# A planner's buffer choice by last reader, copies of x spread over eight blocks, and the next head's loads moved to mid-head, in a one-core hybrid layer

## The chip, the cores and the metric

One program runs on one core of a Trainium2 chip. The metric is the device time of one execution in microseconds (us), lower is better. The engines of the core work side by side: TensorE (PE, with its weight loads PEld), VectorE (DVE), ScalarE (ACT), GpSimd (POOL) and SyncE (SP), which here issues nearly all transfers. Each engine and each queue runs its own instructions strictly in their written order and waits on semaphores where data or a buffer is not ready.

## The reference, cut to what matters

One layer of a decoder over 512 prompt tokens and 64 sample tokens (T = 576 columns), model width 2048, all float32:

```python
proj = x @ w_in + b_in                      # 2048 -> 14352
(s5_u, s5_z, q, k, v, a_low, gla_z, ca, cb, cz, gates) = split(proj)
y_s5  = gelu(s5_mixer(s5_u, ...));  y_s5 = y_s5 * sigmoid(y_s5 @ w_glu + b_glu)
br_s5 = (y_s5 * silu(s5_z)) @ p_s5
o     = gla_mixer(q, k, v, a_low, ...)      # 4 heads, chunked linear attention with decay
br_gla  = (o * silu(gla_z)) @ p_gla
br_conv = (conv_mixer(ca, cb, ...) * silu(cz)) @ p_conv
out = (g_s5 * br_s5 + g_gla * br_gla + g_conv * br_conv) @ w_o     # g = sigmoid(gates)
h = alpha * x + out;  h = h + sigmoid(h @ w_pg) * (p @ w_pe)
return layer_norm(h), the mixers' new states
```

## The kernel before

Activations stand transposed, 128 channels by 576 tokens to a tile. Each large product is made of three products of parts: every operand is split into `hi` (a copy rounded to fp32r, by ACT on line 75) and `lo` (the rest, a subtraction by DVE on line 82), and hi*hi, hi*lo and lo*hi are summed in PSUM, in matmuls of 288 columns (line 435 for plain jobs, 464 for pairs of output blocks that use a seven-product scheme, 547 for the small `w_pe`).

`run_jobs` writes out the work unit by unit; a job is one block of 128 output channels. The order is: eight `s5_u` blocks, the `a` block, ten gate blocks (`NFILL`), 47 pairs for the rest of `w_in`, two quads of `w_pe`, eight `w_glu` blocks, 16 blocks each of `p_s5`, `p_conv` and `p_gla`, eight pairs of `w_o` and 16 blocks of `w_pg`. Weights arrive in four `raw` buffers (lines 352, 375) and, for a part of the pairs, in slots (line 359). Background work is written as Python generators that `pump` advances after each piece of matmuls: the S5 mixer (eight blocks, each `s5_block`, `s5_scan`, `s5_out`), the convolution tiles, the four GLA heads (`gla_head`), and the products y*z (`y_make`). A scheduler then orders each engine's instructions within dependences, so a transfer may be issued well before the place where it is written.

The S5 block b needs a turn through DRAM: line 951 stores a table of kernels to `kd` from a slot that line 970 frees at once, and the sixteen loads of line 967 read it back in a shifted layout for the matmuls of line 1044. Lines 985 and 1040 are the S5 state matmuls before and beside them. `s5_store_u` (line 842 on) empties the PSUM of an `s5_u` block into a slot by ACT and stores it to `ud`.

SBUF is managed as 71 slots of 128x576 (`NSLOT`), named `sl` in the profile. `alloc` takes the slot that stands first in a queue, and `free` puts a slot at its end; `free` is called as soon as the last reader has been written out, which may be a store (to `ud`, `kd`, `gd` for gates, `zd`, `gx` for the convolution's input, `qd` for q, k and v, `cd`, `yd`, `xd` and others). The slot's next writer then waits until that store has landed.

`x_out(k)` copies the k-th transposed block of x to DRAM (`xd`) for its use at the end of the layer: a store of its `hi` part by SP (line 1689), then an adding store of its `lo` part by POOL (line 1690). Eight are written out before the `a` job and eight before the last of the ten gate jobs.

`gla_head(h)` begins with `gla_load` (four transfers from `qd`, line 1238, and two steps of waiting) if its tiles have not been asked for; at the end of head h, line 1397, the tiles of head h + 1 are asked for where more than ten slots are free.

Of the kernel before, what the change touches and what calls it, by code (L numbers as in the profile page):

```python
# [25 lines left out]
NSLOT = 71  # L26
# [19 lines left out]
class K:  # L46
# [10 lines left out]
    def alloc(self, dt=F32):  # L57
        n = 0
        while not self.inbg and (not self.free_slots or n < 300 and self.bg and len(self.free_slots) <= self.reserve):
            self.force()  # L60
            n += 1
            assert n < 5000, ([e[1] for e in self.bg], [e[0].gi_frame.f_lineno for e in self.bg])
        i = self.free_slots.popleft()
        self.cnt += 1
        t = self.slots.tile([128, T], dt, name=f"sl{self.cnt}", tag=f"s{i}")
        self.owner[id(t)] = (i, t)
        return t

    def free(self, *ts):
        for t in ts:  # L70
            i, _ = self.owner.pop(id(t))
            self.free_slots.append(i)

    def act(self, out, in_, func=AF.Copy, **kw):
# [118 lines left out]
    def setup(self):  # L193
        nc, tc, ctx = self.nc, self.tc, self.ctx
        self.const = ctx.enter_context(tc.tile_pool(name="const", bufs=1))
        self.rawp = ctx.enter_context(tc.tile_pool(name="raw", bufs=4))
        self.hip = ctx.enter_context(tc.tile_pool(name="hi", bufs=6))
        self.lop = ctx.enter_context(tc.tile_pool(name="lo", bufs=6))
        self.dram = ctx.enter_context(tc.tile_pool(name="dram", bufs=1, space=DRAM))
        self.ps_mm = ctx.enter_context(tc.tile_pool(name="psmm", bufs=2, space=PSUM))  # L200
        self.ps_two = ctx.enter_context(tc.tile_pool(name="pstwo", bufs=1, space=PSUM))
        self.ps_aux = ctx.enter_context(tc.tile_pool(name="psaux", bufs=2, space=PSUM))
        self.slots = ctx.enter_context(tc.tile_pool(name="slots", bufs=1))
        self.free_slots = deque(range(NSLOT))
# [12 lines left out]
        nc.vector.memset(self.one1, 1.0)  # L217
        self.act(self.one1, self.one1)
# [102 lines left out]
    def run_jobs(self):  # L321
# [126 lines left out]
        def run_pair(u):  # L448
# [38 lines left out]
            if hooks is not None:  # L487
                hooks(p)
            self.pump(BG_PAIR * 3.2)

# [11 lines left out]
        for b, (k0, n) in enumerate(xblocks):  # L502
            g = k0 // HK
            for j in range(2):
                if k0 % HK == 0:
                    prep(2 * g + j)
                if k0 == 0:
                    pss[j] = self.ps_mm.tile([128, 1024], F32, name="mm")
                if j == 1 and b < 4:
                    self.turn_x(*xblocks[b + 1])  # L510
                ka, m, hi, lo = halves[2 * g + j][0]
                mms(pss[j], (k0, n, hi[:, k0 - ka:], lo[:, k0 - ka:]), X, KT, FULL)
                if b > 1:
# [11 lines left out]
        for u in range(first, nu):  # L525
# [11 lines left out]
            if kind == "quad":  # L537
                if before is not None:
                    before()
                xh, xl = xs()  # L540
                hv = halves.pop(u)
                for j in range(4):
                    ps = self.ps_mm.tile([128, 1024], F32, name="mm")
                    for k, (_, _, hi, lo) in enumerate(hv):
                        for lh, rh, a, b in ((hi, xh, k == 0, False), (hi, xl, False, False), (lo, xh, False, k == 1)):
                            for o, c, m in FULL:
                                nc.tensor.matmul(ps[:, o:o + m], lh[:, j], rh[k][:, c:c + m], start=a, stop=b)  # L547
                    evac(j, ps)
                    self.pump(BG_SHORT * 1.6)
                continue  # L550
# [8 lines left out]
            for z, (ka, m, hi, lo) in enumerate(hv):  # L559
                for c in range(0, m, 2):  # L560
                    mms(pss[ji], (ka + c, 2, hi[:, c:], lo if lo is None else lo[:, c:]), xs, nk,
                        PARTS[:1] if dual in (1, 2) else FULL)
                    if z < len(hv) - 1 or c < m - 2:
                        self.pump(rate * 1.6)
            if dual in (1, 2):
                kept.append((ji, xs, hv))
            if k0 + n == nk:
                if dual in (1, 2):
                    evac(pss[ji], 0)
                else:  # L570
                    evac(pss.pop(ji))
                if after is not None:
                    after()
            self.pump(rate * 1.6)
        nm = 0
# [265 lines left out]
    def s5_store_u(self, b, ps):  # L841
# [6 lines left out]
        self.nc.sync.dma_start(self.ud[b], t)  # L848
        self.free(t)
        self.u[b] = True  # L850
# [16 lines left out]
    def s5_block(self, b, st):  # L867
# [83 lines left out]
        nc.sync.dma_start(self.kd[b, :, 128:], kt[:, 128:256])  # L951
        self.free(t)
        if b < 7 and self.u[b + 1] is not None:
# [75 lines left out]
    def s5_out(self, b, st):  # L1029
# [27 lines left out]
        for s in range(8):  # L1057
            nc.sync.dma_start(dst[s], u[16 * s:16 * s + 16].rearrange("c (g n) -> c g n", g=8))
        self.free(t, u)
        yield 2.0  # L1060
# [180 lines left out]
    def gla_head(self, h):  # L1241
# [134 lines left out]
        for a in range(2):  # L1376
# [11 lines left out]
            for z in (2 * a + 1, 2 * a):  # L1388
                nc.gpsimd.dma_start(self.o[8][0, 2 * z:2 * z + 2, h].rearrange("s d v -> d s v"),
                                    s0[z][:, :512].rearrange("p (s v) -> p s v", s=2))  # L1390
                self.free(s0[z])
# [17 lines left out]
        for s in range(2):  # L1409
# [8 lines left out]
            nc.sync.dma_start(self.yd[1, 2 * h + s], y)  # L1418
            self.free(y)
            yield 0.1  # L1420
# [15 lines left out]
    def conv_g(self, n, ca, sig):  # L1436
# [16 lines left out]
        nc.sync.dma_start(self.gx[n, :, 576:880], g2[:, :304])  # L1453
        self.free(g, g2)

# [5 lines left out]
    def conv_tile(self, n):  # L1461
# [19 lines left out]
        nc.gpsimd.dma_start(self.o[9][0, :, 22:30, cs], tmp[:64, 256:384])  # L1481
        self.free(tmp)
        y = self.alloc()
# [20 lines left out]
        nc.sync.dma_start(self.cd[0, n], y)  # L1504
        self.free(y)
        yield 0.7
# [7 lines left out]
    def conv_norm(self):  # L1514
# [17 lines left out]
        for n in range(8):  # L1532
# [9 lines left out]
            nc.sync.dma_start(self.cd[1, n], y)  # L1542
            self.free(y)
            yield 1.4
# [10 lines left out]
        for n in range(8):  # L1555
# [7 lines left out]
            nc.sync.dma_start(self.yd[2, n], y)  # L1563
            self.free(y)
            yield 2.1
# [12 lines left out]
    def br_job(self, name, br, n, y, key, mode, extra=None, order=range(16)):  # L1578
# [20 lines left out]
        def evac(ps):  # L1599
# [6 lines left out]
            else:  # L1606
                self.add(self.A[n], self.A[n], g)
            self.free(g)
        self.job(w, n * 128, lambda: ([a for a, _ in y], [b for _, b in y]), evac, before)
        self.rates[id(self.jobs[-1])] = RATES[name]  # L1610

    def build(self):
# [22 lines left out]
        def evac_a(ps):  # L1635
# [3 lines left out]
            nc.sync.dma_start(self.ad, t)  # L1639
            self.free(t)  # L1640
            self.spawn(self.make_forms(), "forms")
        gates = deque([(1, n) for n in range(16)] + [(0, n) for n in range(16)] + [(2, n) for n in range(16)])

        def gate_one(br, n):
            def evac(ps):
# [3 lines left out]
                nc.sync.dma_start(self.gd[br, n], t)  # L1649
                self.free(t)  # L1650
            self.job(w_in, OFF["gates"] + br * D + n * 128, X, evac)
# [5 lines left out]
        def gate_pair(br, n):  # L1657
            col = OFF["gates"] + br * D + n * 128

            def evac(t0, X0, t1):  # L1660
# [4 lines left out]
                for z, t in enumerate((t0, t1)):  # L1665
                    nc.sync.dma_start(self.gd[br, n + z], t)
                self.free(t0, t1)
            return col, evac

        def z_pair(br, name, n):  # L1670
# [3 lines left out]
            def evac(t0, X0, t1):  # L1674
# [8 lines left out]
                for z, t in enumerate((t0, t1)):  # L1683
                    nc.sync.dma_start(self.zd[br, n + z], t)
                self.free(t0, t1, s0, s1)
            return col, evac
# [93 lines left out]
        def kqv_pair(n, col):  # L1780
            def evac(t0, X0, t1):
# [4 lines left out]
                for z, t in enumerate((t0, t1)):  # L1786
                    nc.sync.dma_start(self.qd[n + z], t)
                self.free(t0, t1)
            return col, evac
# [51 lines left out]
        def pe_quad(m):  # L1841
            def evac(j, ps):
                t = self.alloc()
                self.act(self.s2(t), self.v2(ps))
                nc.sync.dma_start(self.pd[4 * m + j], t)
                self.free(t)
            self.quad_job(self.i["w_pe"][0], 512 * m, parts(P), evac, lambda: self.need("p"))
# [102 lines left out]
        for n in range(0, 16, 2):  # L1950
            def evac(t0, X0, t1, n=n):
# [5 lines left out]
                for k, t in ((n, t0), (n + 1, t1)):  # L1957
                    if n < 12:
                        nc.sync.dma_start(self.hd[k], t)
                        self.free(t)  # L1960
                    else:
                        HL[k] = t
# [330 lines left out]
```

## Time and profile before

| what | value |
|---|---|
| median of three runs | 2302.80 us (2291.73, 2302.80, 2303.48) |
| the profiled execution's own time | 2296.74 us |
| its span, first to last instruction | 2294.8 us |
| PE busy | 2240.8 us, 16892 matmuls |
| DVE / ACT busy | 1797.1 / 1042.0 us |
| SP's queue | 329.16 MB in 422336 packets |
| mean granted clock of PE | 0.990 |

All stages are tables of matmuls with the rest beside them; PE is busy nearly throughout, so what matters is where it stands still and where its clock is halved behind such a halt. Stages by time from the span's start: loading and turning x to about 50 us; plain jobs with the S5 mixer to about 302 us; pairs of `w_in` with the convolution to about 1395 us; `w_glu`, `p_s5`, `p_conv` with the GLA heads to about 1700 us; `p_gla` and `w_o` to about 2045 us; `w_pg` and the layer norm to the end.

### The profile page before, as it was taken

How to read it: one execution, taken by the hardware profiler on the slowest of the kernel's cores; microseconds unless marked ns; L12 is line 12 of the kernel's file. 1: busy time of each engine (PE TensorE's matmuls, PEld its weight loads, DVE VectorE, ACT ScalarE, POOL GpSimd, SP SyncE). 2: the span in 40 equal slices, each digit the busy share in tenths (PEclk: the TensorE clock that was granted, in tenths of full speed). 3: DMA queues.
4: the chain of work that ended last, by engine and by line, in shares of the span. 5: the costliest groups of instructions: out<-in, count | busy, mean ns of one | idle time of the engine just before them, and what ended most of it. 6: DMA issues, size and time to landing. Idle time of an engine off the chain costs nothing.

```text
span 2294.8 us, 44332 instructions
## 1 busy us (share of the span) xinstructions
PE 2240.8 (98%) x16892; PEld 2195.0 (96%) x16892; DVE 1797.1 (78%) x3417; ACT 1042.0 (45%) x2058; POOL 69.7 (3%) x121
## 2 busy tenths in 40 slices
PE   8989999999999999999999999999999999999998
PEld 7979999999999999999999999998989999999996
DVE  6967877989898989999989779865653777774556
ACT  4444444454545455544545556563422334453221
POOL 0010010000000000000000000000110000000000
PEclk9999999999999999999999999999999999999998
DMA  7565574434444443444444467856878444464322
GB/s 214 148 150 133 137 183 140 119 111 137 125 130 120 126 137 119 140 124 131 119 137 123 135 193 261 263 180 191 261 224 219 124 130 141 153 209 130 95 84 83
DMA packets 430005, 348.86 MB, mean 152 GB/s; under 512 B 51198, under 2 KB 368314, under 8 KB 429776
## 3 DMA queue, kind: packets, MB, share of 16 engines
q1 hardware_dynamic: 422336, 329.16, 48.3%
q0 software_dynamic: 7456, 16.88, 3.4%
q8 instruction: 132, 2.16, 0.4%
q14 instruction: 81, 0.66, 0.1%
HBM read 263.74 MB, written 82.89 MB: 151 GB/s over the span
## 4 chain that ended last, share of the span: by engine, by line
PE 83%; issue 6%; DMA 5%; DVE 3%; ACT 2%; SPq 1%; POOL 0%; DVEq 0%; POOLq 0%; ACTq 0%
PE mm L464 30%; PE mm L435 27%; PE aux L464 22%; DVE sl L82 2%; PE mm L547 1%; DMA sl<-in_w_in 1%; PE aux L104 1%; ACT sl L75 1%; DMA kd<-sl 1%; DMA sl<-zd 1%; DVE lo L82 1%; PE two L104 1%; DMA sl<-in_x_prompt 1%; PE two L1040 0%; DVE sl L100 0%
## 5 line engine op out<-in xcount | busy, mean ns | idle before, releaser
L75 ACT ACTIVATE hi<-raw 128x512 fp32r<-128x512 f32 x800 | 501.7, 630 | 669.6 <-PE mm L435 249.1
L435 PE MATMUL mm<-sl,hi 128*128 128x288 f32 (+2 forms) x4000 | 723.1, 300 | 12.7 <-ACT sl L75 9.8
L464 PE MATMUL mm<-sl,hi 128*128 128x288 f32 x3520 | 713.8, 297 | 10.4 <-ACT sl L75 9.3
L82 DVE TENSOR_TENSOR lo<-raw,hi 128x512 fp32r<-128x512 f32 x796 | 547.4, 689 | 208.7 <-ACT hi L75 202.4
L435 PEld LDWEIGHTS mm<-sl,hi 128*128 128x128 f32 x4000 | 595.0, 190 | 20.8 <-ACT sl L75 10.7
L464 PEld LDWEIGHTS mm<-sl,hi 128*128 128x128 f32 x3520 | 567.9, 189 | 12.5 <-ACT sl L75 10.7
L464 PE MATMUL aux<-sl,hi 128*128 128x288 f32 x2640 | 528.1, 294 | 0.3 <-ACT hi L75 0.3
L464 PE MATMUL mm<-sl,lo 128*128 128x288 f32 x1760 | 519.9, 296 | 0.0
L82 DVE TENSOR_TENSOR sl<-sl,sl 128x576 f32<-128x576 f32 (+11 forms) x680 | 369.1, 580 | 93.8 <-ACT sl L75 37.9
L435 PE MATMUL mm<-sl,lo 128*128 128x288 f32 (+2 forms) x1968 | 434.6, 299 | 0.0
L464 PEld LDWEIGHTS aux<-sl,hi 128*128 128x128 f32 x2640 | 421.8, 188 | 0.7 <-ACT hi L75 0.6
L464 PE MATMUL aux<-sl,lo 128*128 128x288 f32 x1320 | 388.6, 294 | 0.8 <-DVE lo L82 0.8
L464 PEld LDWEIGHTS mm<-sl,lo 128*128 128x128 f32 x1760 | 332.4, 189 | 0.1
L435 PEld LDWEIGHTS mm<-sl,lo 128*128 128x128 f32 x1968 | 321.0, 190 | 2.6 <-issue 1.4
L464 PEld LDWEIGHTS aux<-sl,lo 128*128 128x128 f32 x1320 | 247.8, 188 | 1.3 <-DVE lo L82 1.2
L82 DVE TENSOR_TENSOR raw<-raw,sl 128x512 f32<-128x512 f32 x330 | 223.7, 689 | 17.9 <-DMA sl<-in_w_in 17.1
L82 DVE TENSOR_TENSOR lo<-sl,hi 128x512 fp32r<-128x512 f32 x228 | 155.7, 691 | 44.3 <-ACT hi L75 43.4
L75 ACT ACTIVATE hi<-sl 128x512 fp32r<-128x512 f32 x228 | 139.6, 627 | 111.8 <-PE mm L464 77.3
L75 ACT ACTIVATE sl<-sl 128x576 fp32r<-128x576 f32 (+11 forms) x291 | 127.8, 463 | 125.2 <-DVE sl L82 71.6
L100 DVE SCALAR_TENSOR_TENSOR sl<-sl,cw,sl 128x512 f32<-128x512 f32 x240 | 180.0, 750 | 0.2
L75 ACT ACTIVATE sl<-mm 128x288 f32<-128x288 f32 (+3 forms) x146 | 65.9, 451 | 68.0 <-PE mm L464 32.2
L75 ACT ACTIVATE sl<-aux 128x288 f32<-128x288 f32 (+9 forms) x205 | 69.8, 355 | 55.1 <-PE aux L104 34.3
(186 smaller groups left out, 1200.4 us busy)
## 6 DMA issues: line engine op xcount, KB each, us to landing
raw<-in_w_in SPq DMA_DIRECT2D x128, 512.0 KB
sl<-in_w_in SPq DMA_DIRECT2D x196, 256.0 KB
raw<-in_w_pg SPq DMA_DIRECT2D x32, 512.0 KB
gd<-sl SPq DMA_DIRECT2D x48, 288.0 KB
sl<-gd SPq DMA_DIRECT2D x48, 288.0 KB
raw<-in_p_s SPq DMA_DIRECT2D x16, 512.0 KB
raw<-in_p_conv SPq DMA_DIRECT2D x16, 512.0 KB
raw<-in_p_gla SPq DMA_DIRECT2D x16, 512.0 KB
```

The costliest lines, as they stand in the source:

```text
L75: return self.nc.scalar.activation(out, in_, func, **kw)
L82: self.nc.vector.tensor_tensor(out, a, b, op)
L100: self.nc.vector.scalar_tensor_tensor(out, a, s, b, op0=op0, op1=op1)
L104: self.nc.tensor.transpose(out, in_, self.ident[:n, :n])
L435: nc.tensor.matmul(ps[:, o:o + n], lh[:, k - ka], rh[k][:, c:c + n], start=a, stop=b)
L464: nc.tensor.matmul(ps[bank], lh[:, k - ka], rh[k], start=bool(a), stop=b, skip_group_check=not opens)
L547: nc.tensor.matmul(ps[:, o:o + m], lh[:, j], rh[k][:, c:c + m], start=a, stop=b)
```

## The change

Four things are edited. A clock of planned PE time (`self.clock`) is kept while the work is written out, each freed slot gets a time at which its last reader should be done (1.5 us later, or 8.0 us where that reader is a store, `stored`), and `alloc` takes the free slot with the least such time. The sixteen copies of x are written two by two before each of the first eight gate jobs, in place of eight before `a` and eight before the tenth gate job. The loads of the next head's k, q, v are written before the first chunk of a head, where more than 14 slots are free, in place of the head's end, where more than ten are. Nothing is added to or taken from the arithmetic.

```diff
-        i = self.free_slots.popleft()
+        i = min(self.free_slots, key=self.ready.get)
+        self.free_slots.remove(i)
...
-    def free(self, *ts):
+    def free(self, *ts, after=1.5):
+
         for t in ts:
             i, _ = self.owner.pop(id(t))
             self.free_slots.append(i)
+            self.ready[i] = self.clock + after
+
+    def stored(self, *ts):
+
+        self.free(*ts, after=8.0)
...
+        self.ready, self.clock = dict.fromkeys(range(NSLOT), 0.0), 0.0
...
+            self.clock += 3.2
             self.pump(BG_PAIR * 3.2)
...
+                    self.clock += 1.6
                     self.pump(BG_SHORT * 1.6)
...
         self.nc.sync.dma_start(self.ud[b], t)
-        self.free(t)
+        self.stored(t)
...
         nc.sync.dma_start(self.kd[b, :, 128:], kt[:, 128:256])
-        self.free(t)
+        self.stored(t)
...
         nc.sync.dma_start(self.gx[n, :, 576:880], g2[:, :304])
-        self.free(g, g2)
+        self.stored(g, g2)
...
+        if h < 3 and len(self.free_slots) > 14:
+            self.gla_load(h + 1)
         pa = first(0)
...
         if h == 3:
             self.free(*self.gt, self.gm)
-        elif len(self.free_slots) > 10:
-            self.gla_load(h + 1)
...
-        self.job(w_in, OFF["a"], X, evac_a, lambda: [x_out(k) for k in range(8)], dual=3)
-        fill(NFILL)
-        self.jobs[-1] = self.jobs[-1][:5] + (lambda: [x_out(k) for k in range(8, 16)],) + self.jobs[-1][6:]
+        self.job(w_in, OFF["a"], X, evac_a, dual=3)
+        for j in range(NFILL):
+            fill(1)
+            if j < 8:
+                self.jobs[-1] = self.jobs[-1][:5] + (lambda j=j: (x_out(2 * j), x_out(2 * j + 1)),) + self.jobs[-1][6:]
```

The other `free` to `stored` edits are of the same kind (gates, z, `qd`, `cd`, `yd`, `pd`, `hd`, `ad`, the GLA states, and the gated products `g` except in the last branch).

How the instructions move shows at three places. The first is SP's queue around the second S5 block's store to `kd` (slot `sl_1390`; the table is read back into `sl_1528` and `sl_1529`). Before:

```order
L375 DMA raw<-in_w_in 128x8x128 x2
L1689 DMA xd<-sl_81 128x576
L1689 DMA xd<-sl_82 128x576
L1689 DMA xd<-sl_83 128x576
L1689 DMA xd<-sl_84 128x576
L1689 DMA xd<-sl_85 128x576
L1689 DMA xd<-sl_86 128x576
L1689 DMA xd<-sl_87 128x576
L1689 DMA xd<-sl_88 128x576
L375 DMA raw<-in_w_in 128x8x128
L951 DMA kd<-sl_1390 128x128
L375 DMA raw<-in_w_in 128x8x128
```

and in the changed program:

```order
L383 DMA raw<-in_w_in 128x8x128 x3
L874 DMA sl_1061<-in_s_b_re 128x4x16
L383 DMA raw<-in_w_in 128x8x128
L874 DMA sl_1061<-in_s_b_im 128x4x16
L964 DMA kd<-sl_1390 128x128
L383 DMA raw<-in_w_in 128x8x128
L980 DMA sl_1528<-kd 16x4x128
```

Eight copies of x stood ahead of this store; now none does, and the first copy follows the sixteen loads from `kd`. Further on in the changed queue two copies stand ahead of the third block's store to `kd`, three ahead of and two behind the fifth's, two ahead of and three behind the seventh's, and two ahead of the eighth's.

The second place is PE at the same time: the second S5 block's two state products (into PSUM tile `two`, from `sl_1514` and `sl_1515`) and the first block's output products (from `sl_1150`, `sl_1261`), which need what DVE makes of the first block's states. Before:

```order
L104 MATMUL aux<-ident,sl_1397 128x128 x4
L985 MATMUL two<-sl_1231,sl_1514 64x72 x8
L104 MATMUL aux<-ident,sl_1499 128x128 x2
L985 MATMUL two<-sl_1231,sl_1515 64x72 x8
L1040 MATMUL two<-sl_1062,sl_1150 128x144
L1040 MATMUL two<-sl_1063,sl_1151 128x144
L1044 MATMUL two<-sl_1080,sl_1261 128x72 x2
```

and in the changed program (in two pieces, with rows left out between and within them):

```order
L111 MATMUL aux<-ident,sl_1397 128x128 x4
L998 MATMUL two<-sl_1231,sl_1514 64x72 x8
L111 MATMUL aux<-ident,sl_1499 128x128 x2
L443 MATMUL mm<-sl_81,hi 128x288 x2
L443 MATMUL mm<-sl_97,hi 128x288 x2
```

```order
L443 MATMUL mm<-sl_85,hi 128x288 x2
L998 MATMUL two<-sl_1231,sl_1515 64x72 x8
L443 MATMUL mm<-sl_101,hi 128x288 x2
...
L443 MATMUL mm<-sl_90,lo 128x288 x2
L1053 MATMUL two<-sl_1062,sl_1150 128x144
L1053 MATMUL two<-sl_1063,sl_1151 128x144
L1057 MATMUL two<-sl_1080,sl_1261 128x72 x2
```

State and output products stood back to back; now 26 matmuls of a plain job lie between the two state products, and 34 between the second of them and the output products.

The third place is SP where the pairs begin. Before:

```order
L352 DMA raw<-in_w_in 128x4x256
L1689 DMA xd<-sl_89 128x576
L1689 DMA xd<-sl_90 128x576
L1689 DMA xd<-sl_91 128x576
L1689 DMA xd<-sl_92 128x576
L1689 DMA xd<-sl_93 128x576
L1689 DMA xd<-sl_94 128x576
L1689 DMA xd<-sl_95 128x576
L1689 DMA xd<-sl_96 128x576
L359 DMA sl_4440<-in_w_in 128x4x128
L359 DMA sl_4442<-in_w_in 128x4x128
```

and in the changed program:

```order
L1071 DMA yd<-sl_3893 16x8x72 x8
L1663 DMA gd<-sl_4210 128x576
L367 DMA sl_4440<-in_w_in 128x4x128
L360 DMA raw<-in_w_in 128x4x256
L367 DMA sl_4442<-in_w_in 128x4x128
L360 DMA raw<-in_w_in 128x4x256
L367 DMA sl_4515<-in_w_in 128x4x128
```

The last eight copies have left this place for the S5 stage, and the pair's weights follow the stores directly. Of the sixteen copies, ten now stand in SP's queue ahead of the weight load that follows the fifth and sixth blocks' loads from `kd`.

More of the change, by code (lines that the diff above doesn't have):

```diff
@@ L512, in run_jobs @@
                 mms(pss[j], (k0, n, hi[:, k0 - ka:], lo[:, k0 - ka:]), X, KT, FULL)
+                self.clock += 0.8 * n
                 if b > 1:
@@ L563, in run_jobs @@
                     if z < len(hv) - 1 or c < m - 2:
+                        self.clock += 1.6
                         self.pump(rate * 1.6)
@@ L573, in run_jobs @@
                     after()
+            self.clock += 1.6
             self.pump(rate * 1.6)
@@ L1058, in s5_out @@
             nc.sync.dma_start(dst[s], u[16 * s:16 * s + 16].rearrange("c (g n) -> c g n", g=8))
-        self.free(t, u)
+        self.free(t)
+        self.stored(u)
         yield 2.0
@@ L1390, in gla_head @@
                                     s0[z][:, :512].rearrange("p (s v) -> p s v", s=2))
-                self.free(s0[z])
+                self.stored(s0[z])
             yield 1.4
@@ L1418, in gla_head @@
             nc.sync.dma_start(self.yd[1, 2 * h + s], y)
-            self.free(y)
+            self.stored(y)
             yield 0.1
@@ L1481, in conv_tile @@
         nc.gpsimd.dma_start(self.o[9][0, :, 22:30, cs], tmp[:64, 256:384])
-        self.free(tmp)
+        self.stored(tmp)
         y = self.alloc()
@@ L1504, in conv_tile @@
         nc.sync.dma_start(self.cd[0, n], y)
-        self.free(y)
+        self.stored(y)
         yield 0.7
@@ L1542, in conv_norm @@
             nc.sync.dma_start(self.cd[1, n], y)
-            self.free(y)
+            self.stored(y)
             yield 1.4
@@ L1563, in conv_norm @@
             nc.sync.dma_start(self.yd[2, n], y)
-            self.free(y)
+            self.stored(y)
             yield 2.1
@@ L1607, in evac @@
                 self.add(self.A[n], self.A[n], g)
-            self.free(g)
+            self.free(g, after=1.5 if mode == "last" else 8.0)
         self.job(w, n * 128, lambda: ([a for a, _ in y], [b for _, b in y]), evac, before)
@@ L1639, in evac_a @@
             nc.sync.dma_start(self.ad, t)
-            self.free(t)
+            self.stored(t)
             self.spawn(self.make_forms(), "forms")
@@ L1649, in evac @@
                 nc.sync.dma_start(self.gd[br, n], t)
-                self.free(t)
+                self.stored(t)
             self.job(w_in, OFF["gates"] + br * D + n * 128, X, evac)
@@ L1666, in evac @@
                     nc.sync.dma_start(self.gd[br, n + z], t)
-                self.free(t0, t1)
+                self.stored(t0, t1)
             return col, evac
@@ L1684, in evac @@
                     nc.sync.dma_start(self.zd[br, n + z], t)
-                self.free(t0, t1, s0, s1)
+                self.free(s0, s1)
+                self.stored(t0, t1)
             return col, evac
@@ L1787, in evac @@
                     nc.sync.dma_start(self.qd[n + z], t)
-                self.free(t0, t1)
+                self.stored(t0, t1)
             return col, evac
@@ L1845, in evac @@
                 nc.sync.dma_start(self.pd[4 * m + j], t)
-                self.free(t)
+                self.stored(t)
             self.quad_job(self.i["w_pe"][0], 512 * m, parts(P), evac, lambda: self.need("p"))
@@ L1959, in evac @@
                         nc.sync.dma_start(self.hd[k], t)
-                        self.free(t)
+                        self.stored(t)
                     else:
```

## The prediction

> **What bounds the kernel now.** I read the page's totals first, then the table by stretches of time, then the waits that ended PE's halts, and last SP's queue in those stretches.
>
> ```profile
> span 2294.8 us, 44332 instructions
> PE 2240.8 (98%) x16892; PEld 2195.0 (96%) x16892; DVE 1797.1 (78%) x3417; ACT 1042.0 (45%) x2058; POOL 69.7 (3%) x121
> ```
>
> PE is busy for 2240.8 of 2294.8 us, and the change takes no matmul away. So it can win at most PE's halts, 54 us, and the time in which the clock is low behind them. The table by stretches (us; busy time of PE, PEld, DVE, ACT, POOL; granted clock, DMA share, GB/s) shows where the halts are that the edits touch:
>
> ```profile
> 100.00:120.00 20.00, 20.00 (x160) 19.27 (x159) 18.40 (x45) 5.43 (x13) 4.34 (x7) 1.00 0.81 226
> 120.00:136.00 16.00, 7.24 (x79) 6.50 (x78) 5.46 (x17) 3.27 (x10) 2.89 (x4) 0.94 1.07 219
> 136.00:144.00 8.00, 8.00 (x45) 8.00 (x46) 4.76 (x14) 7.03 (x17) 0.00 (x0) 0.70 0.38 99
> 152.00:200.00 48.00, 47.79 (x431) 45.02 (x424) 38.51 (x90) 21.45 (x60) 0.58 (x1) 1.00 0.55 124
> 340.00:352.00 12.00, 9.05 (x65) 8.41 (x64) 9.06 (x19) 3.98 (x9) 0.00 (x0) 1.00 1.02 294
> 352.00:362.00 10.00, 10.00 (x66) 10.00 (x65) 4.92 (x8) 4.03 (x8) 0.12 (x1) 0.83 0.37 95
> 430.00:450.00 20.00, 17.42 (x133) 17.19 (x132) 18.69 (x33) 9.51 (x19) 1.06 (x2) 1.00 0.56 163
> 1570.00:1585.00 15.00, 12.90 (x83) 11.94 (x82) 4.63 (x11) 4.32 (x12) 0.00 (x0) 0.89 0.70 213
> ```
>
> The worst is 120 to 136 us: PE works 7.24 us of 16, while the DMA engines are full (share 1.07), and behind it the granted clock is 0.70. The second, 340 to 352, also has full DMA engines.
>
> **Copies of x, first eight.** SP's and POOL's queues around the halt (start, length, queue, line, transfer), with the next block's store for comparison, and the waits from 118 to 140 us:
>
> ```profile
> 109.61 7.22 SPq L1689 DMA_DIRECT2D xd<-sl  x8
> 115.66 7.27 POOL L1690 DMA_DIRECT2D xd<-sl  x8 [69.37 <-DVE sl L82]
> 119.75 0.34 SPq L951 DMA_DIRECT2D kd<-sl  x1
> 134.65 7.45 SPq L967 DMA_DIRECT2D sl<-kd  x16
> 155.73 0.34 SPq L951 DMA_DIRECT2D kd<-sl  x1
> 157.33 8.10 SPq L967 DMA_DIRECT2D sl<-kd  x16
> ...
> ACT sl L75 <- DMA kd<-sl: 11.1, 1, 11.1
> PE mm L435 <- ACT sl L75: 6.7, 1, 6.7
> PE two L1040 <- DVE sl L82: 1.9, 1, 1.9
> ```
>
> Sixteen transfers stand ahead of the `kd` store of 119.75, and its loads start 14.9 us later; without copies ahead (155.73) it is 1.6 us. The store's slot has already been given to the next `s5_u` block, so ACT cannot empty that block's PSUM for 11.1 us, and PE waits 6.7 us for the PSUM. Two edits remove this wait, each alone enough: no copy stands ahead of this store any more, and a stored slot counts as busy 8 us from its release. I take all 6.7, and the clock behind it: 8 us at 0.70 is 2.4. PE's other halt here, 1.9 for DVE's states, stood between products that followed each other at once; 26 and 34 matmuls now separate them, at 20 us to 160 (the first row) 3.3 and 4.3 us, so I take the 1.9 too. Together 11.0. The loads of the second block start 13 us earlier, and SP is free that long; what is late next there is DVE, 18.40 of 20 us busy just before.
>
> **Copies of x, second eight.**
>
> ```profile
> 318.01 6.87 SPq L1689 DMA_DIRECT2D xd<-sl  x8
> 324.99 9.18 SPq L359 DMA_DIRECT2D sl<-in_w_in  x4
> ...
> DVE raw L82 <- DMA sl<-in_w_in: 10.6, 2, 7.8
> PE mm L464 <- ACT sl L75: 2.1, 1, 2.1
> PE aux L464 <- DVE lo L82: 0.8, 1, 0.8
> ```
>
> The pair's weights are issued behind eight copies, DVE waits 10.6 us for them and PE 2.9 us for DVE and ACT. In the new order the weights follow the `yd` and `gd` stores at once, 6.87 us earlier. I take 2.9, and 10 us at 0.83, 1.7: together 4.6.
>
> On this clock the Trainium skill ("TensorE: Matmul & The Clock Gate", Why this matters for your kernels) says that halts of more than about 3 us should be avoided, since one idle window halves the clock. By that rule the halt here, 2.9 us in two parts, need not cost the 1.7, and the sum below would be 19.6 in place of 21.3. The rows show 0.83 behind it, and 1.00 in 430 to 450 with a halt of 2.6; the measured loss stands in the sum.
>
> **The slot whose reader ends first.** Beside the first halt, the waits for stores that reach PE are these (from 440 to 447, 533 to 539 and 200 to 206 us):
>
> ```profile
> ACT sl L75 <- DMA gx<-sl: 1.5, 1, 1.5
> PE mm L464 <- ACT sl L75: 2.6, 1, 2.6
> ...
> PE mm L464 <- ACT sl L75: 1.9, 1, 1.9
> ...
> DVE sl L82 <- DMA gd<-sl: 3.1, 1, 3.1
> PE aux L104 <- DVE sl L82: 1.2, 1, 1.2
> ```
>
> After a `cb` pair the next pair's first PSUM is emptied into the slot of a `gx` store written out 3.2 us of planned PE time before; six slots are free there. With 8.0 us on the stored ones, the other free slots go first. Counted through the code's takes and frees, the reuses of a stored slot within 6 us of plan fall from 19 to 10, and none is left at these places; what stays is in the norm of the convolution and at the first `w_o` pair, where nothing else is free. I take 2.6 + 1.9 + 1.2 = 5.7. Plain slots are taken sooner in turn: the shortest new reuses are an S5 block's read-back tables, into slots that PE's transposes have just read. Those transposes stand right behind the `kd` store in PE's order, and the loads wait 1.6 us for the store anyhow, so I cost that at nothing; if PE runs late there, SP waits, and with it the weights.
>
> **What the copies cost in their new place.** SP issues eight in 7.22 us, 0.9 each beside other transfers, and the S5 stage already has one stretch without a weight load, from 202.20 to 240.28, filled by the loads of two blocks:
>
> ```profile
> 202.20 1.12 SPq L375 DMA_DIRECT2D raw<-in_w_in  x2
> 240.28 2.30 SPq L375 DMA_DIRECT2D raw<-in_w_in  x3
> ...
> ACT hi L75 <- DMA raw<-in_w_in: 11.2, 1, 11.2
> PE two L1040 <- ACT sl L75: 2.7, 1, 2.7
> ```
>
> There ACT stands 11.2 us on a late weight, the S5 work queued behind it is late, and PE waits 2.7. In the new order two copies fall into that stretch, 1.8 us, and eight stand ahead of it; but one weight load more is issued before it (the 25th against the 24th, counted in both queues). The bounds: a gain of 2.7 if the additional load covers the stretch; a loss of 9.0 if all ten delay the weight, and 2.4 for the clock. I take a loss of 1.8, nearest to the two copies that lie inside. POOL's adding stores wait for SP's as before; POOL is busy 69.7 us in all, and nobody waits for `xd` until `w_o`.
>
> **The next head's loads.** Counted in the same way, 14 or fewer slots are free before the first chunk of heads 0 and 1, so the mid-head load is not written there; with the load at the head's end gone, heads 1 and 2 now load at their own start, one step later in the code than before. Only head 3 is fetched mid-head. The scheduler issues loads early all the same: in SP's queue the last load of head 1 stands one weight load later than before, that of head 2 behind as many as before, that of head 3 one earlier. The waits at 1575 to 1583 and 1681 to 1687 us show what is at stake:
>
> ```profile
> ACT sl L75 <- DMA sl<-qd: 4.9, 1, 4.9
> PE aux L1325 <- ACT sl L75: 2.1, 1, 2.1
> ...
> DVE sl L82 <- DMA sl<-zd: 4.8, 1, 4.8
> PE two L1326 <- ACT sl L75: 3.5, 1, 3.5
> ```
>
> ACT reaches head 2's first piece of work 4.9 us before its tile lands, and head 1's products behind it halt PE for 2.1 (and 15 us at 0.89, 1.7). The other halt is for `zd`, which is not moved. The bounds are a gain of 3.8 and, if the same comes at head 1 also, a loss of 3.8; I take nothing, the middle, since the last loads keep their places within one weight load.
>
> **The sum.** 11.0 + 4.6 + 5.7 = 21.3, less 1.8, is 19.5. From the profiled execution, 2296.7, that is 2277; from the median of the runs shown, 2302.8, it is 2283. The runs lie at 2291.7, 2302.8 and 2303.5, the profiled one between them. I forecast 2282. About 0.5% (11.5 us) can be told from no change.
>
> **Rivals.** *The wait goes where the copies go.* The copies move the same bytes, now in a stage that is full: SP is behind from 202 to 240, DVE had 18.40 of 20. Then the 15.6 of the two bursts comes back as late weights and late S5 work in small pieces, and only 5.7 is won: 2302.8 - 5.7 = 2297. For it speak ACT's 11.2 us wait without any copy near; against it that from 152 to 200 us PE was busy for 47.79 of 48, and that the DMA engines, full in both bursts, had a share of 0.55 there. The Trainium skill ("DMA: Bandwidth & Descriptors", Issuing engines are not separate DMA queues) would speak for it: transfers of all issuing engines run on the same 16 DMA engines and interleave, so a copy costs its time wherever it is issued from. In the rows above the cost came from the queue at one moment, a share of 1.07.
>
> *Slower: a block's turn through `kd` halts PE again.* Four later blocks have two to five copies around their store. If each halts PE as the second block did, 4 x (6.7 + 2.4) = 36.4 is lost against 21.3 won: 2302.8 + 15.1 = 2318. It decides when copies hold the store longer than PE's work between the block's kernel product and its output products, 171 to 201 matmuls in the new order, at 0.125 us some 21 to 25 us. Eight copies held it 14.9 - 1.6 = 13.3 us, 1.7 each, so five hold it 8.3; and the slot is no longer given away. It is unlikely.
>
> *The new choice of slots does nothing* (other stores come late, or the next slot is as bad): 5.7 stays lost, and the copies alone give 11.0 + 4.6 - 1.8 = 13.8: 2289.
>
> **How the numbers follow.** The sum as worked out has 0.55, all of it below 2291 but 0.02; the slots without effect 0.10, half of it below 2291; the wait that moves with the copies 0.25, of which 0.05 ends below 2291 and the rest within 0.5%; the slower case 0.10. So faster 0.63, same 0.27, slower 0.10. The low end adds the gains left out, 2.7 and 3.8, to the sum from the profiled time: 2277 - 6.5, about 2271. The high end takes in the rival at 2297 and stops below the slower case: 2301. The likeliest alone ranges from 2271 to 2292, with the losses of 9.6 above what I took (11.4 - 1.8) at its upper end.
>
> **What would show it.** Right: no wait of ACT for `kd` of 11 us and no PE halt of 6.7 between 110 and 140 us; `kd` loads some 2 us behind their store; a granted clock of 1.00 from 100 to 170 and from 340 to 370; no PE wait behind `gx`; `raw` and slot weights at the first pair without 10.6 us of DVE waiting. Wrong: ACT waiting for `raw<-in_w_in` at several places between 150 and 300 us with PE behind it; a block's line-1057 products waiting for SP; new waits for `qd` at the start of heads 1 and 2; or halts of the same size among pairs, where the new choice of slots reorders the work of ACT and DVE.

## The result and the profile after

The changed kernel takes 2280.7 us (median of six runs, 2276.1 to 2282.1), the kernel before in the same job 2294.1 (2290.9 to 2303.5). The ratio is 0.9930, with a 95% interval of 0.9907 to 0.9954: faster by 13 us between the medians, or by 0.7% by the ratio, where 2282 was forecast. That the time came so near is in part luck. A forecast of 2282 with a gain of 19.5 starts at 2301.5, for which three runs were known; six runs put the start at 2294.1, and the gain is smaller than the sum: 13.4 us between these medians, 16.7 between the two profiled spans, 17.8 in the later job of e11_after, where the start was 2297.0. One term of the sum failed, and most of the experiments below are about that one.

The profiled execution took 2280.1 us. Its head, and the table by stretches of time (busy time of PE, PEld, DVE, ACT, POOL; granted clock, DMA share, GB/s). The first four rows cover the same times as those of before, the next three the places that were 340 to 352, 352 to 362 and 430 to 450 there:

```profile
span 2278.1 us, 44359 instructions
...
PE 2234.5 (98%) x16892; PEld 2192.4 (96%) x16892; DVE 1795.0 (79%) x3417; ACT 1041.9 (46%) x2058; POOL 69.3 (3%) x121
```

```profile
100.00:120.00 20.00, 20.00 (x161) 19.28 (x160) 17.94 (x45) 6.37 (x17) 0.00 (x0) 1.00 0.55 135
120.00:136.00 16.00, 15.88 (x145) 15.24 (x144) 11.39 (x28) 7.65 (x27) 1.97 (x2) 1.00 0.69 177
136.00:144.00 8.00, 8.00 (x75) 7.29 (x74) 7.16 (x14) 5.18 (x11) 0.00 (x0) 1.00 0.81 161
152.00:200.00 48.00, 45.44 (x399) 43.39 (x400) 39.99 (x92) 22.76 (x66) 2.28 (x3) 0.96 0.61 142
338.00:350.00 12.00, 12.00 (x93) 12.00 (x92) 5.46 (x9) 6.51 (x12) 0.00 (x0) 1.00 0.24 68
350.00:360.00 10.00, 10.00 (x78) 10.00 (x76) 8.10 (x14) 4.46 (x9) 0.12 (x1) 1.00 0.38 107
419.00:439.00 20.00, 20.00 (x154) 20.00 (x153) 19.57 (x36) 10.67 (x21) 1.06 (x2) 1.00 0.65 187
```

The three places where the prediction saw a gain are full now: PE is busy 15.88 of 16 us where it was 7.24, and 12.00 of 12 and 20.00 of 20 at the first pair and behind the first `gx` store, all at a clock of 1.00. The fourth row is the other side: between 152 and 200 us PE was busy 47.79 of 48 at 1.00 before, and is 45.44 at 0.96 now. SP's queue shows the first turn through `kd` as forecast, the loads 2.2 us behind the store, and a later one that is worse than before:

```profile
118.38 0.34 SPq L964 DMA_DIRECT2D kd<-sl  x1
120.16 0.37 SPq L383 DMA_DIRECT2D raw<-in_w_in  x1
120.58 1.77 SPq L980 DMA_DIRECT2D sl<-kd  x3
...
202.78 0.38 SPq L964 DMA_DIRECT2D kd<-sl  x1
203.20 0.44 SPq L874 DMA_DIRECT2D sl<-in_s_b_im  x1
203.69 0.50 SPq L1704 DMA_DIRECT2D xd<-sl  x1
204.23 1.64 SPq L383 DMA_DIRECT2D raw<-in_w_in  x2
205.91 2.23 SPq L1704 DMA_DIRECT2D xd<-sl  x1
208.26 0.37 SPq L874 DMA_DIRECT2D sl<-in_s_b_re  x1
208.72 10.58 SPq L980 DMA_DIRECT2D sl<-kd  x16
```

Two copies and two weights stand between the store of 202.78 and its loads, which follow 5.9 us behind it. The waits from 180 to 240 us (total, times, longest) say what they hold up:

```profile
ACT sl L82 <- DMA kd<-sl: 8.3, 2, 5.1
...
DVE sl L89 <- DMA sl<-in_s_b_im: 5.0, 1, 5.0
...
PE aux L111 <- DMA sl<-in_s_c_re: 3.3, 1, 3.3
...
PE aux L958 <- DVE sl L89: 2.2, 1, 2.2
```

ACT stands at slots whose `kd` store is still on its way, DVE and PE at inputs that were issued late. To see where time is won and given back, the next table follows PE's matmuls of 288 columns, 15,280 in each kernel: for some of them, the start in the trace less its start in the trace of before, in us (negative is earlier). Number 576 stands ahead of the first halt, 768 behind it and behind the low clock that followed it before. 1216 lies within the S5 stage. 1792 is the first of the first pair, 2000 lies behind that pair's halts, 3300 behind both `gx` halts (which stood at 2512 and 3184), 9600 ahead of the first head, 15270 near the end. At these places every kernel has the same other matmuls behind it (e2_copies has 48 small ones more at 1216). At 672, the place of the first halt itself, that is not so: 48 of S5's products, some 4.5 us of PE's work, stood ahead of it before and stand behind it in the changed kernel.

| kernel | 576 | 768 | 1216 | 1792 | 2000 | 3300 | 9600 | 15270 |
|---|---|---|---|---|---|---|---|---|
| changed kernel | -1.1 | -12.1 | +0.1 | -3.3 | -8.4 | -13.0 | -14.9 | -15.1 |
| changed kernel, second trace (e11_after) | -0.7 | -11.8 | +2.2 | -1.1 | -6.3 | -10.8 | -13.2 | -13.4 |
| e1_slot: slots alone | -0.2 | -3.7 | -2.8 | -5.9 | -9.2 | -13.8 | -17.2 | -20.5 |
| e2_copies: copies alone | -0.3 | -10.9 | +10.1 | +6.2 | +1.0 | +2.5 | +0.1 | -1.0 |
| e3_gla: heads' loads alone | +0.2 | +0.3 | +1.1 | +0.8 | +0.5 | +0.2 | -1.7 | -2.8 |
| e10_late_old: old slots, copies late | +0.4 | -10.2 | -7.3 | -9.1 | -14.3 | -14.5 | -16.3 | -17.1 |
| e5_late: new slots, copies late | +0.5 | -10.6 | -7.1 | -5.3 | -10.5 | -15.1 | -18.5 | -18.8 |
| e9_late_rate | -0.3 | -11.3 | -7.9 | -10.3 | -15.5 | -20.6 | -23.7 | -26.4 |
| e8_rate | +0.2 | -10.8 | -1.0 | +4.3 | -0.3 | -5.1 | -8.4 | -15.2 |
| e4_double: copies twice | -0.6 | -11.7 | +7.1 | +26.5 | +21.9 | +17.1 | +13.5 | +17.6 |
| e12_pool: copies issued by POOL | -0.6 | -11.6 | -3.9 | +3.1 | -2.1 | -6.6 | -9.5 | -14.9 |

In the changed kernel the first halt's end is worth 11.0 us (from -1.1 to -12.1), and 8.9 of them are given back before the first pair. (Differences here and below are taken before rounding.) The second trace of the same kernel stood 2.2 us later at 1792 and 1.7 later at 15270, so differences of two or three us in one column mean nothing. The traced runs of e1_slot, e8_rate and e10_late_old are 3 to 7 us faster than the medians of their kernels, so their rows flatter them.

### The profile page after: what moved, and what is told of

Its sections match the earlier page's. It is cut to its first block, busy times and chain, and to the rows that moved or that the text cites. A ratio compares the mean times of both kernels' runs of the same rounds, so it can differ in the third digit from the quotient of the medians.

```text
span 2278.1 us, 44359 instructions
## 1 busy us (share of the span) xinstructions
PE 2234.5 (98%) x16892; PEld 2192.4 (96%) x16892; DVE 1795.0 (79%) x3417; ACT 1041.9 (46%) x2058; POOL 69.3 (3%) x121
## 4 chain that ended last, share of the span: by engine, by line
PE 85%; DMA 6%; DVE 4%; issue 2%; ACT 2%; SPq 1%; POOL 0%; DVEq 0%; ACTq 0%; POOLq 0%
PE mm L472 30%; PE mm L443 28%; PE aux L472 22%; DVE sl L89 2%; ACT sl L82 1%; PE mm L557 1%; DMA yd<-sl 1%; DMA sl<-gd 1%; PE aux L111 1%; PE two L111 1%; DMA xd<-sl 1%; DMA sl<-yd 1%; DVE lo L89 1%; DMA sl<-in_x_prompt 1%; PE two L1053 1%
## 5 line engine op out<-in xcount | busy, mean ns | idle before, releaser
L89 DVE TENSOR_TENSOR sl<-sl,sl 128x576 f32<-128x576 f32 (+12 forms) x680 | 367.8, 577 | 97.1 <-ACT sl L82 43.5
L82 ACT ACTIVATE sl<-aux 128x288 f32<-128x288 f32 (+10 forms) x205 | 69.9, 354 | 55.0 <-PE aux L111 28.1
```

The lines of the kernel that those rows point to most:

```text
L82: return self.nc.scalar.activation(out, in_, func, **kw)
L89: self.nc.vector.tensor_tensor(out, a, b, op)
```

## The experiments

**The edits apart: e1_slot, e2_copies, e3_gla.** Each is the kernel before with one edit of the change, word for word as in the diff above.

> The kernel before with the new choice of slots alone; the copies stay in two bursts and the heads' loads as before. Theory A (the choice of slots removes the first halt by itself, and the copies' new place costs 11 us in the S5 stage): ACT no longer waits 11 us for kd near 123 us, PE wins the 13 us there and some 5 behind gx, nothing is lost between 150 and 250 us, the halt at the first pair (2.9 and the clock) stays: 2294 - 18 = 2276, faster than the changed kernel. Theory B (the first halt needs the copies moved, since the kd loads behind them come late all the same): only the gx halts go, 2294 - 5 = 2289. Theory C (the loss in the S5 stage comes from the choice of slots, through plain slots taken sooner): the S5 stage loses 11 here too, 2294 - 18 + 11 = 2287.

> The kernel before with the copies spread over eight blocks alone; slots are taken in the old order, the heads' loads as before. Theory A (the copies cost 11 us in the S5 stage): the first halt goes (-13), the first pair's goes (-4), the S5 stage loses 11, the gx halts stay: 2294 - 6 = 2288. Theory C (the S5 loss comes from the choice of slots): no loss between 150 and 250 us, 2294 - 17 = 2277.

> The kernel before with the edit of the heads' loads alone (mid-head when more than 14 slots are free, no load at the head's end). My step: no effect, since heads 1 and 2 load at their own start and their last loads keep their places within one weight load: 2294 to 2298, the median of before within 2. Rival (the later loads cost a halt more at a head's start): 3.8 us slower, with ACT waiting for qd at heads 1 and 2.

| kernel | median us | ratio to before | 95% interval |
|---|---|---|---|
| e1_slot | 2277.3 | 0.9912 | 0.9897 to 0.9928 |
| e2_copies | 2296.6 | 0.9998 | 0.9985 to 1.0011 |
| e3_gla | 2293.4 | 0.9986 | 0.9972 to 1.0000 |

The slots alone win 20 us, at least as much as the whole change; the copies alone win nothing. Each alone removes the 6.7 us halt, as the prediction said, but they are not worth the same: at matmul 768 the copies' edit has won 10.6 us and the slots' 3.5. In e1_slot the copies still stand ahead of the second block's `kd` store, and its loads follow 13.5 us behind it. SP's queue in e1_slot, and the waits from 118 to 140 us:

```profile
119.73 0.34 SPq L964 DMA_DIRECT2D kd<-sl  x1
133.22 8.39 SPq L980 DMA_DIRECT2D sl<-kd  x16
```

```profile
DVE sl L89 <- DMA sl<-in_s_b_im: 9.3, 1, 9.3
PE two L1053 <- ACT hi L82: 4.8, 1, 4.8
```

ACT's wait of 11.1 for `kd` is gone, yet the queue is as late as it was: DVE waits 9.3 for an input of the next block, and PE 4.8 at the state products. From there to the first pair e1_slot loses nothing more. At the first pair it wins 3.3 us, though the copies still stand there, and 4.5 where the `gx` halts were. In e2_copies the first halt's 10.6 and the first pair's 5.2 are won, but 17.1 are lost between the two, and the `gx` halts stay. Its queue, and its waits from 160 to 200 us:

```profile
166.99 0.58 SPq L1689 DMA_DIRECT2D xd<-sl  x1
168.09 0.66 SPq L1689 DMA_DIRECT2D xd<-sl  x1
168.85 1.71 SPq L375 DMA_DIRECT2D raw<-in_w_in  x2
170.61 2.33 SPq L1689 DMA_DIRECT2D xd<-sl  x2
173.04 0.40 SPq L951 DMA_DIRECT2D kd<-sl  x1
173.48 3.81 SPq L375 DMA_DIRECT2D raw<-in_w_in  x2
179.31 12.67 SPq L967 DMA_DIRECT2D sl<-kd  x16
```

```profile
PE two L1044 <- DMA sl<-kd: 3.3, 1, 3.3
...
PE two L985 <- ACT sl L75: 3.1, 1, 3.1
```

Four copies go ahead of the `kd` store of 173.04, its loads come 6.3 us behind it and take 12.67 us (8.39 in e1_slot), and PE waits for them itself. Theory A held in direction for both, but not in size: it gave e1_slot the whole first halt and e2_copies a loss of 11. Theory C falls, for e1_slot has the new slots and no loss of that kind. The heads' loads alone come out 3 us faster, at the edge of what can be told, and their trace has only 1.1 of that behind matmul 9600, where the heads begin. ACT's waits for `qd`, 8.5 us among the heads before, do not occur in that trace; in the changed kernel 5.5 of them do.

**What the copies cost: e4_double, e5_late, e10_late_old, e12_pool.** e4_double adds to `x_out` a second pair of stores:

```
+            self.pin(nc.sync.dma_start(self.xe[k], self.xh[k].bitcast(F32)))
+            nc.gpsimd.dma_start(self.xe[k], self.xl[k].bitcast(F32), accum_op=OP.add)
```

e5_late and e10_late_old move the copies to a later place, with the new and with the old slots; e12_pool issues the storing copy elsewhere. "Late" is not wholly out of the S5 stage: in e5_late the first copy goes out at 244.79 us, past matmul 1216, four go ahead of the last block's `kd` store at 273.10, and eight wait for the pairs. The edit for the late copies and then that of e12_pool (`...` stands for code left out):

```
-            if j < 8:
-                self.jobs[-1] = ... (lambda j=j: (x_out(2 * j), x_out(2 * j + 1)),) ...
+            if j > 5:
+                self.jobs[-1] = ... (lambda j=j: (x_out(2 * j - 12), x_out(2 * j - 11)),) ...
...
+            elif 8 <= j < 16:
+                bef = lambda j=j: x_out(j)
```

```
-            self.pin(nc.sync.dma_start(self.xd[k], self.xh[k].bitcast(F32)))
+            self.pin(nc.gpsimd.dma_start(self.xd[k], self.xh[k].bitcast(F32)))
```

> The changed kernel with each of the 16 copies written twice (the second store and its adding store go to a second scratch tensor that nobody reads), so the spread copies' load on the queues and the DMA engines doubles at the same places. Theory A (16 copies in the S5 stage cost 11 us): another 11 or more, 2281 + 11 = 2292, with more waits of ACT for raw weights and of PE behind them between 150 and 330 us. Theory C (copies there cost nothing, the loss is the slots'): 2281 within 2.

> The changed kernel with the copies out of the S5 stage: the eight whose tiles the first pair overwrites stand two each at the last four gate blocks before the pairs, the other eight one each at pairs 8 to 15, where the DMA engines have a share of about 0.4. Theory A (the copies cost 11 us in the S5 stage): most of it is won back, 2281 - 9 = 2272, faster than both kernels. Theory C (the loss is the slots'): 2281 within 2. Rival (the loss follows the copies wherever they go): 2281 to 2285, with halts at pairs 8 to 15.

> The kernel before, slots in the old order, with the copies placed as in e5_late (eight at the last four gate blocks, eight at pairs 8 to 15). With e2_copies it tells what the copies cost in the S5 stage when slots are taken in the old order. Theory A (in the old order the copies alone cause the first halt, and their place among the S5 blocks costs as much as that): the first halt is gone (-13 at 140 us), half of it is handed back by 330 us, the first pair's halt is gone, the gx halts stay: 2296 - 10 = 2286, 10 below e2_copies. Theory B (the old order hands back everything wherever the copies are): 2296 within 3.

> The changed kernel with the 16 storing copies issued from POOL's queue, where their adding stores already stand, in place of SP's; same bytes, same blocks. Theory A (a copy costs in the S5 stage because it stands in SP's queue ahead of the kd loads and weights): SP is as free as in e5_late and the 6 us between the two come back, 2280 - 5 = 2275. Theory B (it costs because its bytes share the DMA engines with the loads of S5): the place of issue does not matter, 2280 within 3.

| slots | copies in two bursts | among the S5 blocks | late |
|---|---|---|---|
| old order | 1 (before) | 0.9998 (0.9985 to 1.0011) | 0.9944 (0.9923 to 0.9964) |
| by last reader | 0.9912 (0.9897 to 0.9928) | 0.9930 (0.9907 to 0.9954) | 0.9900 (0.9883 to 0.9917) |

(The changed kernel, second row and middle, also has the edit of the heads' loads, and so has e5_late; the others have not.) With the old slots the copies cost 0.54% more among the S5 blocks than late, 12 us, and the intervals are apart. With the new ones it is 0.3%, some 7 us, and the intervals overlap a little. Written twice (1.0059, 1.0043 to 1.0074; 2311.3 us) they cost 30 us more than written once: the price climbs with their number. So theory A held in these three runs, in e4_double with more than the 11 us that it named. In that trace weights come late eight times, and once a block's output products wait for their loads from `kd`, the slower rival's place (from 140 to 330 us):

```profile
ACT hi L82 <- DMA raw<-in_w_in: 22.0, 8, 10.8
...
PE two L1057 <- DMA sl<-kd: 6.8, 1, 6.8
```

e12_pool asked whether it is their place in SP's queue. Its ratio is 0.9922 (0.9894 to 0.9949; 2280.0 us), the changed kernel's own, as theory B said. The Trainium skill ("DMA: Bandwidth & Descriptors", Issuing engines are not separate DMA queues) says that transfers of all issuing engines run on the same 16 DMA engines, and that another issuer saves only the time of issuing; the time agrees, though the trace does not show that shared engines are the reason. SP has more free time and spends it waiting (first fence, from 100 to 330 us; 5.2 in the changed kernel), and ACT still stands at `kd` (second, from 100 to 345; 11.8 there):

```profile
SPq L383 <- DVE lo L89: 17.1, 6, 8.9
```

```profile
ACT sl L82 <- DMA kd<-sl: 21.1, 3, 9.4
```

Up to matmul 1216 e12_pool is 4.0 us ahead of the changed kernel. One halt, behind ACT's wait of 9.4 for a `kd` store, takes that back (from 244 to 266 us):

```profile
PE two L998 <- ACT sl L82: 7.0, 1, 7.0
```

The edit also moved the copies in time: POOL, which takes its work in order, issues the first at 170.58 us, where SP issued it at 129.10 in the changed kernel. So taking the copies off SP's queue won nothing over the whole program; whether it is their bytes that cost stays open.

**How long a stored slot should count as busy: e6_stored20, e7_late20.** The changed kernel and e5_late with

```
-        self.free(*ts, after=8.0)
+        self.free(*ts, after=20.0)
```

> The changed kernel with 20 us in place of 8 for a slot that a store still reads. Counted through the takes and frees, reuses of a stored slot within 15 us of plan fall from 38 to 20, and in the S5 stage none within 14 us is left (seven or so with 8 us). Theory A (what the first halt's end wins is handed back in the S5 stage because ACT takes slots whose kd and yd stores stand far behind in SP's queue): ACT's waits for kd<-sl between 140 and 260 us, 11.8 us in three, go, and with them some 6 us of PE halts and clock: 2281 - 6 = 2275. Theory B (the S5 stage is held by the late loads behind the copies, and those waits are only where it shows): the waits move to other lines, 2281 within 2.

> The kernel with the copies out of the S5 stage (e5_late) and 20 us for stored slots. Theory A: ACT's waits there for yd<-sl (9.2 us) and kd<-sl (5.6 us) go, and PE's halts at 199 and 222 us with them, 4.5 us and the clock behind: 2275 - 6 = 2269, faster than every kernel so far. Theory B (PE runs ahead of the S5 chain of DVE, ACT and SP however the slots are dealt): the halts stay with other waits in front of them, 2275 within 2.

Theory A fell in both. e6_stored20 takes 2295.6 us, a ratio of 0.9999 (0.9988 to 1.0011): all of the gain is lost. e7_late20 takes 2281.4, 0.9941 (0.9922 to 0.9959), 0.4% behind e5_late. The waits that were aimed at shrink, and others grow (e6_stored20 from 100 to 345 us, ACT's waits and then one of SP's; the changed kernel has 27.4 in the first, 11.8 in the second and 5.6 in three in the third):

```profile
ACT sl L82 <- DVE sl L89: 48.9, 24, 7.9
...
ACT sl L82 <- DMA kd<-sl: 2.4, 1, 2.4
```

```profile
SPq L1663 <- ACT sl L82: 14.0, 2, 13.5
```

When the S5 stage has taken a slot, some 8 are left free on average and 3 at the least, counted in the code's own takes. If the stored ones are kept back, ACT gets slots that DVE has barely left, and SP, which takes its stores in order, stands 13.5 us behind one of them. What 8 us does well is a balance between two waits, not the removal of one.

**Whether PE runs into the S5 chain: e8_rate, e9_late_rate.** The changed kernel and e5_late with less S5 work written per us of PE:

```
-BG_RATE, BG_SHORT, BG_PAIR = 1.25, 0.5, 0.27
+BG_RATE, BG_SHORT, BG_PAIR = 1.15, 0.5, 0.27
```

> The changed kernel with BG_RATE, the S5 and forms work written per us of planned PE time in the gate blocks, at 1.15 in place of 1.25. Written so, the S5 work still ends before the first pair (19 us of plan earlier with 1.25, 3 us with 1.15). Theory A (with the first halt gone PE runs into the S5 chain of DVE, ACT and SP, and halts there in small pieces; at 1.25 one and a half gate blocks at the end have no S5 work beside them): the halts between 150 and 230 us, 10.5 us, fall by half, and the low clock behind them: 2281 - 6 = 2275. Theory B (each order of the S5 stage has its own collisions in slots and in SP's queue, and the rate has no part in them): no gain that follows the rate, 2281 within 5 either way.

> The kernel with the copies out of the S5 stage (e5_late) and BG_RATE 1.15. Theory A: its five halts between 171 and 252 us, 10.2 us, fall by half: 2275 - 5 = 2270, the fastest. Theory B: 2275 within 5 either way.

> The changed kernel once more, on the chip of these runs, as their yardstick: 2281 within 3. If e1_slot and e5_late (0.991 and 0.990 of before) are truly faster than it, its ratio stays at 0.993 or above.

The changed kernel again gave 2279.2 us, 0.9926 (0.9902 to 0.9950). e8_rate is no better: 2288.9, 0.9958 (0.9939 to 0.9976). e9_late_rate took 2269.9, 0.9880 (0.9854 to 0.9906), and its slowest run, 2270.9, lies below the fastest of the changed kernel's on that chip, 2275.1. Its S5 stage has one halt of more than 1 us where e5_late has five, and it reaches the first pair 5 us earlier. PE's waits for ACT, first in e5_late from 140 to 260 us, then in e9_late_rate from 140 to 331:

```profile
PE two L998 <- ACT sl L82: 7.9, 5, 2.0
...
PE two L1053 <- ACT sl L82: 1.2, 1, 1.2
```

```profile
PE two L998 <- ACT sl L82: 3.3, 1, 3.3
```

So theory A held with the copies late. With the copies among the S5 blocks it fell, and theory B's 2281 within 5 was missed too. That e9_late_rate beats e5_late (2275.0) is likely, but their intervals overlap. It is the fastest version of the study, and clearly faster than the kernel before.

## Why the prediction was right, and which steps failed

The time was met within 1.3 us because two errors met: a start taken too high (2301.5, against 2294.1 in the same job and 2297.0 in a later one) and a gain taken too large (19.5, against 13.4 and 17.8). Of the terms, three came out and one did not.

*The first halt: right in place, mechanism and size, 11.0 forecast, 11.0 measured* (10.6 to 11.0 in every row of the table that moves the copies). The 11 us wait for `kd` and the halts of 6.7 and 1.9 are gone, and the clock is 1.00 from 100 to 170 us, as forecast. That each of the two edits alone removes the 6.7 us was right too. Wrong was to take the two as equal: with the slots alone the loads stay late, another halt of 4.8 comes, and only 3.5 us are won.

*What the copies cost in their new place: the step that failed.* The prediction took a loss of 1.8, from 0.9 us of SP's time for each of two copies. From behind the first halt to the first pair 8.9 us were given back, 10.7 in the second trace, near the far end of the bounds (9.0 and 2.4). PE's waits there sum to 9.8 us against 4.1 before, and its clock is 0.97 against 1.00 (from 136 to 340 us, before from 144 to 341). Two things are in it. The copies' place is 3.5 to 5.3 of it by the traces (8.9 and 10.7 against the 5.3 that e5_late gives back over the same matmuls) and some 7 us by the ratios of whole runs, 12 with the old slots. It is not SP's time alone, since e12_pool without it is no faster. The other 5.3 are there with the copies late. They may come from PE reaching S5's products before ACT, DVE and the loads have them ready: PE waits 9.1 us for ACT in e5_late, and with fewer S5 steps per us of PE only 1.0 is given back (e9_late_rate). But the same edit does not help where the copies stand among the S5 blocks (e8_rate), so this part is likely and not shown. Nor is it told apart whether the new slots have a share: with the old ones e10_late_old gives back 1.1, but in a traced run 6 us faster than its median. Either way the sum counted the end of a halt in full, although the stage behind it could not keep it. The sign that the prediction named for a loss was ACT at late weights; in the changed kernel that is 0.7 us between 140 and 260, and the waits are those for `kd` stores and S5's inputs.

*The first pair and the slots: right in size.* From 1792 to 2000 the changed kernel wins 5.2 us, where 4.6 was forecast, and every other row that moves the copies has 4.6 to 5.2 there. That e1_slot wins 3.3 with the copies in place was not foreseen. From 2000 to 3300 it wins 4.5, as forecast for the `gx` halts (2.6 + 1.9); e1_slot wins 4.5 and e5_late 4.7, while e2_copies loses 1.5 and e10_late_old wins 0.2, so this is the slots' work. The 1.9 won from 3300 to 9600 belong to no edit: e3_gla, which is the kernel before up to the heads, wins as much there. The shares of the two edits were wrong all the same. The forecast had 13.8 for the copies and 5.7 for the slots; measured alone, over the whole program, the copies bring 0 (-2.5 to 3.4), since the S5 stage takes back what the two halts give, and the slots 20 (17 to 24). Of the 20.5 that the trace of e1_slot wins, 6.8 lie behind matmul 3300, where the forecast named nothing, and their cause is open.

*The balance.* The terms' errors are 0.0 at the first halt, -8.2 in the S5 stage (8.9 lost, where 1.8 lost and the 1.2 of the `gd` halt won were forecast), +0.6 at the first pair and 0.0 at the `gx` halts. With the 1.9 and another 2.9 at the start and the end of the program, which no edit was meant to move, they leave a gain of 16.7 in the span, of the 19.5 summed.

*The heads' loads: nothing forecast, nothing found in the changed kernel* (-14.9 at 9600, -15.1 at 15270). What they won alone is within the bound of 3.8.

*The rivals.* "The wait goes where the copies go" describes what e2_copies did: 15.8 won at the two halts, 17.1 lost among the S5 blocks, with a late weight of 10.9 and PE's halts of 2.0 to 3.3 as its small pieces. That its 2296.6 is near the rival's 2297 is chance, since the rival starts at 2302.8 and counts 5.7 for the slots. In the changed kernel it is half true. "The new choice does nothing" is refuted by e1_slot. The slower rival did not come, but e4_double shows that it is near: twice the copies, and a block's turn through `kd` halts PE for 6.8 us.

## What to carry to other kernels

A removed halt is worth what the stage behind it can take: before counting it in full, look at how long PE ran there without a wait, and at how full the engines are that feed it. When a wait for a buffer is moved by choosing another buffer, name who read that one last; with few free buffers each choice trades a wait for a store against a wait for an engine. Measure edits that touch one halt one by one, and measure the start as often as the change: a total that comes out can hide an error in both. When two programs are compared at a fixed instruction, choose one that has the same work behind it in both.

## What the runs showed of the hardware

The clock after a short halt does not follow from the halt's length alone. In the changed kernel a halt of 1.7 us, from 172.4, is followed by about 3.4 us at 0.50 to 0.58; in e5_late one of 1.9 us, from 171.9, is followed by none (rows by stretches, first the changed kernel):

```profile
172.00:174.20 2.20, 0.50 (x6) 0.26 (x8) 1.42 (x7) 2.20 (x7) 0.04 (x1) 1.00 0.28 55
...
175.90:177.60 1.70, 1.70 (x9) 1.70 (x9) 1.08 (x4) 0.88 (x6) 0.00 (x0) 0.50 1.21 309
177.60:179.30 1.70, 1.70 (x10) 1.70 (x10) 1.70 (x6) 0.00 (x0) 0.00 (x0) 0.58 0.67 107
179.30:181.00 1.70, 1.70 (x15) 1.70 (x15) 1.38 (x3) 0.63 (x1) 0.00 (x0) 1.00 0.23 60
```

```profile
170.00:174.00 4.00, 2.14 (x32) 1.66 (x32) 2.48 (x10) 2.88 (x10) 0.58 (x1) 1.00 0.95 235
174.00:178.00 4.00, 3.96 (x42) 3.81 (x39) 3.13 (x8) 1.91 (x9) 0.00 (x0) 1.00 1.15 306
178.00:182.00 4.00, 4.00 (x36) 4.00 (x34) 3.90 (x10) 0.41 (x1) 0.00 (x0) 1.00 0.53 148
```

Of e5_late's later halts, two of 2.0 us (from 199.1 and 222.6) left the clock at 1.00, and one of 1.8, from 251.9, was followed by 0.57 for 4 us. The Trainium skill ("TensorE: Matmul & The Clock Gate", Why this matters for your kernels) warns of halts above some 3 us; these runs show the loss behind halts of 1.7 and 1.8 us, not each time. The same page of the Trainium skill, in Part 1: The HAM clock gate, says that the clock follows activity in a window of about 3.4 us that runs free of the kernel. The length of the low stretch agrees, and so would the chance in it; a halt of 2 us cannot fill such a window, though. What decides it stays open.
